# Output product of a hybrid layer: the residual x added by accumulating transfers, the final weight in S1's room, row sums prepared ahead of the last square

## The chip, the cores and the metric

The kernel runs on one core of a Trainium2 chip. The metric is the device time of one execution in microseconds (us). TensorE (PE in the profile) multiplies, VectorE (DVE) and ScalarE (ACT) work elementwise, GpSimd (POOL) and SyncE (SP) mostly issue transfers here. Transfers are issued into queues by SP, ACT and POOL and carried out by 16 DMA engines that all queues share.

## The reference, cut to what matters

One encoder layer: two branches (a Mamba-2 scan and a latent attention), merged by gates, then an output product, the residual and a final RMSNorm. The change touches only the last lines:

```
merged = jax.nn.sigmoid(g_ssm) * (y @ w_proj_ssm) + jax.nn.sigmoid(g_attn) * (o @ w_proj_attn)
x = x + merged @ w_out
...
y = xf * lax.rsqrt(jnp.mean(xf * xf, axis=-1, keepdims=True) + EPS)
return (y * w.astype(jnp.float32)).astype(x.dtype)
```

x and the output have 512 rows (tokens) and 2048 columns, float32.

## The kernel before

All large products are made in split precision: an operand is stored as a high part (rounded to the multiplier's format) and a low part (the remainder), and one product is three matmuls, high by high, high by low and low by high. For weights, ScalarE makes the high part `wh` (L433) and VectorE the low part `wl` (L434), chunk by chunk of 128 x 1024, three buffers deep. So each chunk that TensorE uses needs one ScalarE and one VectorE instruction before it.

The output is made in 128 x 512 tiles, named (t, b): t = 0 to 3 is the block of rows, b = 0 to 3 the block of columns. Columns b = 0 and 1 are multiplied plainly (the loop at L1607 and after). Columns b = 2 and 3 are made by a Strassen scheme (`Strassen.pair`, here called `wo`), with seven products in the order P1, P5, P6, P2, P3, P7, P4. Each is 48 matmuls of 128 x 512 over two banks of PSUM and four weight chunks (m = 0 to 3). Their operands are m's quarters x11, x12, x22 and the sums S1 to S4. P1 uses x11, P5 S1, P6 S2, P2 x12, P3 S4, P7 S3 and P4 x22. X and Y are the weight chunks of the quarter columns, kept and added to: `X<-wo` and `Y<-wo` from POOL's queue are accumulating transfers (L505), which add what they read from memory to what lies in the tile.

What the products leave is combined on VectorE in a tile `big` (parts "p1", "p5", "u", "C12", two tiles each). When P2 has been made, tiles (0, 2) and (1, 2) are complete in p1 (L653). After P3, (0, 3) and (1, 3) are complete in C12 (L630). After P7, (2, 3) and (3, 3) are complete in p5 (L625), and u gets its last addend but one (L728). P4, whose weights are split whole and kept (`keep`), gives (2, 2) and (3, 2) one after the other: first the matmuls of row block 2, then those of 3.

A complete tile goes through `done_o`: the tile of x is added (L1640), the square is summed by ScalarE into `ssf` (L1573), and for t = 2 and 3 the final weight is multiplied in early (`weigh`, L1570). For t = 0 and 1 the tiles of x are loaded by POOL's queue into buffers `gate` ahead of the product (L1628); for t = 2 and 3 they lie, with the final weight, in the tile `fw`, which is loaded by ACT's queue (L1646 and L1649) when P2 is done, in the room that x12 gives up. When a row block is complete, `finish` (L1651) sums its four squares (L1653), scales (L1654), makes the reciprocal root with one Newton step (L185 to L191, one operation on ScalarE and five on VectorE), scales its four tiles and issues their stores.

The program order of each engine is fixed when the kernel is built: TensorE runs in the order of the code, the other engines in an order that a scheduler chooses by priority and data dependences. An engine executes its instructions in order and stops at one whose inputs are not there. Functions hung on a product's name (`hook`) are put into the program when that product has been written down.

Of the kernel before, what the change touches and what calls it, by code (L numbers as in the profile page):

```python
# [18 lines left out]
P = 128  # L19
D = 2048  # L20
# [52 lines left out]
def build(tc, a):  # L73
# [27 lines left out]
    def few(n):  # L101

        n_small[0] += n
        assert n_small[0] <= 96
        return small[:, n_small[0] - n:n_small[0]]
# [275 lines left out]
    def st(name):  # L381
        return gp.tile([P, SEQ], F32, tag="st", bufs=3, name=name)
# [179 lines left out]
    def product(name, op, chunk, extra=None, pre=None):  # L562

        used.append((used[-1] + 1) % 4)
        bs = [b(name) for b in SETS[used[-1]]]
        for m in range(4):
            raw = chunk(m)
            h, l = w_split(raw)
            if extra:
                extra(m, raw)  # L570
            if pre and m == 2:
                pre()
            for i in range(2):
                for jj in range(2):
                    j = 2 * m + jj
                    xh, xl = op(0, j, i), op(1, j, i)
                    wh, wl = (t[:, jj * 512:(jj + 1) * 512] for t in (h, l))
                    pe.matmul(bs[i], xh, wh, start=(j == 0), stop=False)  # L578
                    pe.matmul(bs[i], xh, wl, start=False, stop=False)  # L579
                    pe.matmul(bs[i], xl, wh, start=False, stop=(j == 7))  # L580
                    yield 3
        product_done()
        return bs
# [19 lines left out]
    class Strassen:  # L603
# [60 lines left out]
        def pair(self, cp, headed=False):  # L664
            w, made = self.w, self.made
            X, Y = self.ahead.pop(cp, []), []

            def column(m):
                if m == len(X):
                    X.append(self.columns(w_tile("X"), cp, m))  # L670
                return X[m]

            if headed:
                p1 = self.p1[cp]
            else:
                p1 = evict((yield from product(
                    "P1", self.op("x11"), (lambda m: w_load(w_tile("X"), w, cp, 0, 0, m)) if made else column,
                    None if made else lambda m, raw: w_more(raw, w, cp, 0, 1, m))), "p1", self.tile_)
                self.hook(cp, "P1")

            def c5(m):
                column(m)
                Y.append(w_load(w_tile("Y"), w, cp, 1, 1, m))
                return X[m]

            T3 = []

            def c7(m):
                if made and not T3:
                    T3.extend(t_load(w_tile("Y"), w, cp, "T3", i) for i in range(4))  # L690
                return T3[m] if made else Y[m]

            def t2(m, raw):
                with tc.high_priority(offset=AHEAD):
                    dve.tensor_add(raw, raw, Y[m])

            def t4(m, raw):
                with tc.high_priority(offset=AHEAD):
                    dve.tensor_add(X[m], X[m], raw)

            def t4_alone(m, raw):
                raw = w_tile("w")
                tc.keep_in_program_order(nc.sync.dma_start(raw, a[w][cp, 1, 0, m]))
                t4(m, raw)

            p5 = evict((yield from product("P5", self.op("S1"), c5, t2)), "p5", self.tile_)
            self.hook(cp, "P5")
            A = yield from product("P6", self.op("S2"), lambda m: X[m])
            u = p1 if headed else [self.tile_("u", i) for i in range(2)]
            for i in range(2):  # L710
                dve.tensor_add(u[i], p1[i], A[i])
                self.minus_r(p5[i], p5[i], u[i])
            self.hook(cp, "P6")
            if not headed:
                yield from self.second(cp, p1, lambda i: p1[i], t4)
                self.hook(cp, "P2")
            B = yield from product("P3", self.op("S4"), lambda m: Y[m], None if made else lambda m, raw: w_more(raw, w, cp, 0, 1, m),
                                   self.pre(0, 2 * cp + 1))
            for i in range(2):
                o = sum_tile("ms") if headed else self.tile_("C12" if self.last else "p1", i)  # L720
                self.r_sum(o, p5[i], B[i])
                self.done(i, 2 * cp + 1, o)
            self.hook(cp, "P3")
            A = yield from product("P7", self.op("S3"), c7, t4_alone if headed else None, self.pre(2, 2 * cp + 1))
            for i in range(2):
                self.minus_r(p5[i], p5[i], A[i])
                self.done(2 + i, 2 * cp + 1, p5[i])
                dve.tensor_add(u[i], u[i], A[i])  # L728
            self.hook(cp, "P7")
            if self.last:  # L730
                yield from self.last("P4", self.op("x22"), lambda m: X[m], u)
                return
            A = yield from product("P4", self.op("x22"), lambda m: X[m], None, self.pre(2, 2 * cp))
            for i in range(2):
                self.r_sum(u[i], u[i], A[i])
                self.done(2 + i, 2 * cp, u[i])
            self.hook(cp, "P4")
# [139 lines left out]
    def rsqrt1(v):  # L877

        return small_rsqrt(v, 1, lambda n: hi.tile([P, 1], F32, tag={"rt": "mx", "rr": "nm"}[n], bufs=4, name=n))
# [487 lines left out]

    n_places = [0]

    def place(shape, name):  # L1370

        n = n_places[0] % 5
        n_places[0] += 1
        return xb.tile(shape, F32R, tag="opb" if n else "opc", bufs=4 if n else 1, name=name)

    def slot(which):
        if which in ("x11", "x12"):
# [173 lines left out]
    def x_of(t, b):  # L1551
        return a["x"][t * P:(t + 1) * P, b * SEQ:(b + 1) * SEQ]
# [13 lines left out]
        return w_split(w_load(w_tile("w"), "wo", 0, kc // 4, cg, kc % 4))  # L1566

    def weigh(t, b):
        if t >= 2 and b != 2:
            dve.tensor_mul(res[t, b], res[t, b], room["fw"][:, b])  # L1570

    def squares(t, b):
        act.activation(st("scr"), res[t, b], AF.Square, accum_out=ssf[:, t, b:b + 1])  # L1573

    def m_sums(q):
        ks = slice(4 * q, 4 * q + 4)
# [45 lines left out]
    m_place("S4")()  # L1622
    m_split("S4")()

    def fetch_o(t, b):
        if t < 2:
            fetched[t, b] = st("gate")
            pool.dma_start(fetched[t, b], x_of(t, b))  # L1628

    def kept_o(tag, i):  # L1630
        if "big" not in room:
            room["big"] = xa.tile([P, 4, 2, SEQ], F32, tag="opa", bufs=2, name="big")
        return room["big"][:, ("p1", "p5", "u", "C12").index(tag), i]

    def x_late(t, b):
        return fetched[t, b] if t < 2 else room["fw"][:, 2 * (b - 2) + 2 + t]

    def done_o(t, b, o):
        res[t, b] = o
        dve.tensor_add(o, o, x_late(t, b))  # L1640
        squares(t, b)
        weigh(t, b)

    def final_weights():
        t_ = room["fw"] = xa.tile([P, 8, SEQ], F32, tag="opa", bufs=2, name="fw")
        act.dma_start(t_[:, 0:4], a["fnw"].rearrange("o (b n) -> o b n", b=4).broadcast_to([P, 4, SEQ]))  # L1646
        for t in (2, 3):
            for b in (2, 3):
                act.dma_start(x_late(t, b), x_of(t, b))  # L1649

    def finish(t):  # L1651
        v = few(1)
        dve.tensor_reduce(v, ssf[:, t, :], AX.X, ALU.add)  # L1653
        dve.tensor_scalar(v, v, 1.0 / D, EPS, ALU.mult, ALU.add)  # L1654
        r = rsqrt1(v)
        for b in (2, 0, 1, 3):
            o = res[t, b]
            if b == 2 or t < 2:
                dve.scalar_tensor_tensor(o, o, r, room["fw"][:, b], ALU.mult, ALU.mult)
            elif b == 1 or b == 2:  # L1660
                dve.tensor_scalar_mul(o, o, r)
            else:
                act.activation(o, o, AF.Copy, scale=r)
            (nc.sync if t < 3 or b % 2 == 0 else act).dma_start(a["out"][t * P:(t + 1) * P, b * SEQ:(b + 1) * SEQ], o)

    def last_o(name, op, chunk, u):
        keep = [place([P, 4, 1024], f"keep{i}") for i in range(2)]

        def before():
            for i in range(2):  # L1670
                dve.tensor_add(u[i], x_late(2 + i, 2), u[i])

        def each(i, bank):
            res[2 + i, 2] = u[i]
            with tc.high_priority(offset=12 * i):
                dve.tensor_add(u[i], u[i], bank)
                squares(2 + i, 2)
            finish(2 + i)

        yield from product_rows(name, op, chunk, keep, each, before)  # L1680

    wo = Strassen("wo", m_ops, 1, done_o, fetch_o, {
        (1, "P2"): [final_weights],
        (1, "P3"): [lambda: [weigh(t, b) for t in (2, 3) for b in (0, 1)], lambda: finish(0)],
        (1, "P7"): [lambda: finish(1)]}, kept_o, last_o)
    used.extend([0, 0, 3])
    run(wo.pair(1))
    manual.__exit__(None, None, None)
# [68 lines left out]
```

## Time and profile before

| | |
|---|---|
| median of the three runs shown | 2021.59 us (2018.48 to 2027.99) |
| the profiled execution | 2028.84 us |
| its span, first to last instruction | 2027.1 us |
| mean granted TensorE clock | 0.991 |
| TensorE busy | 1951.1 us (96%) |
| VectorE busy | 1523.9 us (75%) |
| ScalarE busy | 985.2 us (49%) |
| POOL busy | 318.6 us (16%) |
| first matmul of P7 | starts at 1988.14 us |
| last matmul (of P4) | starts at 2016.39 us |
| last store issued | 2022.20 us |

A row of a timeline has the start, the duration, the engine, the line, the operation, the tile written and the tiles read. Square brackets give the time for which the engine had been idle and what ended that. A row of a windows view has, for a stretch of time, the busy us of PE, its weight loads, DVE, ACT and POOL with their counts, then the granted clock, the share of time for which the DMA engines were busy, and GB/s.

### The profile page before, as it was taken

Reading aid. Unit: us, or ns where it says so; the run is one execution under the profiler, and the core shown is the slowest. Engines: PE = TensorE matmul, PEld = TensorE weight load, DVE = VectorE, ACT = ScalarE, POOL = GpSimd, SP = SyncE. Lnnn points to the kernel's source line nnn. Section 1 sums busy time; section 2 is a strip of 40 time slices with the busy share of each in tenths; the row PEclk is TensorE's granted clock in tenths of the full one; section 3 lists DMA queues with packets and bytes.
Section 4 is the critical chain, followed back from the end, with each engine's and each line's share of the span. In section 5 each row is a group of like instructions: output and inputs, shape, how many; then the busy total and the mean of one; then the engine's idle time right before and its main releaser. Section 6 shows DMA issues by size and latency. Waiting matters only on the chain.

```text
span 2027.1 us, 24730 instructions
## 1 busy us (share of the span) xinstructions
PE 1951.1 (96%) x9026; PEld 1610.9 (79%) x9026; DVE 1523.9 (75%) x2010; ACT 985.2 (49%) x1370; POOL 318.6 (16%) x353
## 2 busy tenths in 40 slices
PE   6999999999999999999999999999999999999996
PEld 5888888888878778787788878887877787888885
DVE  7976676676759879899787577666676898879376
ACT  6444445444444655646546444444455455444353
POOL 0001001001032242243331101110011111100010
PEclk9999999999999999999999999999999999999999
DMA  5468558558456747686574857883279787847436
GB/s 192 166 186 208 159 132 208 158 134 208 125 172 170 233 144 209 215 243 201 168 200 149 245 158 197 206 222 94 72 216 301 221 289 281 285 151 244 156 63 176
DMA packets 168650, 382.77 MB, mean 189 GB/s; under 512 B 16272, under 2 KB 65552, under 8 KB 168336
## 3 DMA queue, kind: packets, MB, share of 16 engines
q1 hardware_dynamic: 103248, 233.61, 35.5%
q0 software_dynamic: 29824, 102.25, 22.8%
q10 hardware_dynamic: 35456, 45.33, 6.3%
q8 instruction: 71, 1.16, 0.2%
q14 instruction: 51, 0.42, 0.1%
HBM read 329.22 MB, written 98.04 MB: 211 GB/s over the span
## 4 chain that ended last, share of the span: by engine, by line
PE 60%; DVE 17%; issue 10%; DMA 8%; ACT 3%; POOL 1%; SPq 0%; DVEq 0%; POOLq 0%; ACTq 0%
PE P L579 9%; PE P L580 9%; PE P L578 9%; PE za L168 2%; PE za L169 2%; PE za L170 2%; DVE sum L1052 2%; DVE wl L434 2%; PE xbc L168 2%; PE xbc L169 2%; PE xbc L170 2%; DVE wl L164 2%; DMA wraw<-wps 1%; PE pb L1329 1%; PE qkv L170 1%
## 5 line engine op out<-in xcount | busy, mean ns | idle before, releaser
L433 ACT CAST wh<-X 128x1024 fp32r<-128x1024 f32 x164 | 172.3, 1053 | 197.1 <-PE P L580 149.9
L434 DVE TENSOR_TENSOR wl<-X,wh 128x1024 fp32r<-128x1024 f32 x164 | 199.8, 1222 | 90.5 <-ACT wh L433 90.1
L164 DVE TENSOR_TENSOR wl<-wraw,wh 128x1024 fp32r<-128x1024 f32 (+2 forms) x148 | 176.7, 1195 | 85.4 <-ACT wh L163 83.2
L163 ACT CAST wh<-wraw 128x1024 fp32r<-128x1024 f32 (+2 forms) x150 | 145.1, 969 | 134.2 <-PE xbc L169 39.5
L434 DVE TENSOR_TENSOR wl<-Y,wh 128x1024 fp32r<-128x1024 f32 x88 | 107.3, 1222 | 68.6 <-ACT wh L433 68.6
L168 PE MATMUL xbc<-h_h,wh 128*128 128x512 f32 x384 | 152.8, 398 | 0.0
L433 ACT CAST wh<-Y 128x1024 fp32r<-128x1024 f32 x88 | 92.6, 1054 | 123.4 <-PE P L580 105.5
L169 PE MATMUL xbc<-h_l,wh 128*128 128x512 f32 x384 | 150.8, 393 | 0.0
L170 PE MATMUL xbc<-h_h,wl 128*128 128x512 f32 x384 | 150.7, 392 | 0.0
L578 PE MATMUL P<-wh,h_h 128*128 128x512 f32 x384 | 149.4, 389 | 0.0
L579 PE MATMUL P<-wl,h_h 128*128 128x512 f32 x384 | 149.4, 389 | 0.0
L580 PE MATMUL P<-wh,h_l 128*128 128x512 f32 x384 | 149.4, 389 | 0.0
L434 DVE TENSOR_TENSOR wl<-wraw,wh 128x1024 fp32r<-128x1024 f32 x68 | 83.1, 1221 | 63.3 <-ACT wh L433 63.2
L433 ACT CAST wh<-wraw 128x1024 fp32r<-128x1024 f32 x68 | 71.6, 1053 | 115.9 <-PE P L580 61.8
L579 PE MATMUL P<-wl,S 128*128 128x512 f32 x288 | 112.3, 390 | 0.3 <-DVE wl L434 0.2
L578 PE MATMUL P<-wh,S 128*128 128x512 f32 x288 | 112.1, 389 | 0.0
L580 PE MATMUL P<-wh,S 128*128 128x512 f32 x288 | 112.0, 389 | 0.0
L168 PE MATMUL za<-h_h,wh 128*128 128x512 f32 x256 | 101.4, 396 | 0.0
L169 PE MATMUL za<-h_l,wh 128*128 128x512 f32 x256 | 99.9, 390 | 0.0
L170 PE MATMUL za<-h_h,wl 128*128 128x512 f32 x256 | 99.9, 390 | 0.0
L1052 DVE TENSOR_TENSOR_SCAN sum<-da,scn 128x512 f32<-128x512 f32 x64 | 86.2, 1360 | 0.0
L170 PEld LDWEIGHTS xbc<-h_h,wl 128*128 128x128 f32 x384 | 72.9, 190 | 15.7
(737 smaller groups left out, 5200.5 us busy)
## 6 DMA issues: line engine op xcount, KB each, us to landing
wraw<-wi SPq DMA_DIRECT2D x102, 512.0 KB, 4.2
T_wps<-wps POOLq DMA_DIRECT2D x32, 512.0 KB, 6.3
da<-da_d SPq DMA_DIRECT2D x64, 256.0 KB, 4.5
T_wpa<-wpa POOLq DMA_DIRECT2D x32, 512.0 KB, 9.4
wraw<-wps SPq DMA_DIRECT2D x24, 512.0 KB, 6.0
wraw<-wo SPq DMA_DIRECT2D x20, 512.0 KB, 3.5
xbc_d<-xbc ACTq DMA_DIRECT2D x24, 256.0 KB, 3.0
wraw<-wun SPq DMA_DIRECT2D x16, 384.0 KB, 3.2
```

What stands on the lines that cost most here:

```text
L163: act.copy(h, raw)
L164: (dve if ahead[0] else pool).tensor_sub(l, raw, h.bitcast(F32))
L168: pe.matmul(out, wh, xh, start=start, stop=False)
L169: pe.matmul(out, wh, xl, start=False, stop=False)
L170: pe.matmul(out, wl, xh, start=False, stop=stop)
L433: i = act.copy(hi_, raw)
L434: dve.tensor_sub(lo_, raw, hi_.bitcast(F32))
L578: pe.matmul(bs[i], xh, wh, start=(j == 0), stop=False)
L579: pe.matmul(bs[i], xh, wl, start=False, stop=False)
L580: pe.matmul(bs[i], xl, wh, start=False, stop=(j == 7))
L1052: dve.tensor_tensor_scan(sums[dd], flat(da), mask, 0.0, ALU.add, ALU.mult)
L1329: pe.transpose(tp[:, k * P:(k + 1) * P], prs[t][:, k * P:(k + 1) * P], ident)
```

## The change

Four things change, all in the output product.

1. x is no longer loaded into tiles of its own and added on VectorE. An accumulating transfer of POOL's queue adds it in the parts themselves (`x_added`): into p1 and u after P6, into C12 and p5 after P3. A part holds its final value only with P2's, P7's or P4's banks, so for p1, u and p5 x is in before the last addend; C12 is complete before x comes.
2. The final weight `fw` is loaded after P5 into the room that S1 gives up, by itself. The second half of P4's kept weights moves into x12's room, which is free after P2.
3. The weighing of tiles (2, 0), (3, 0), (2, 1), (3, 1) moves from after P3 to after P2, and `finish` of row blocks 0 and 1, two calls now together, to the last chunk of P7.
4. For row blocks 2 and 3 three of the four squares are summed, scaled and given EPS before the last square (`most`); the last square then goes straight into the root on ScalarE as its input, with `most` as bias. The Newton step takes four VectorE operations instead of five.

```
+            def late(m, raw):
+                if m == 3:
+                    self.hook(cp, "P7a")
...
-    def fetch_o(t, b):
-        if t < 2:
-            fetched[t, b] = st("gate")
-            pool.dma_start(fetched[t, b], x_of(t, b))
...
+    def x_added(tag, t0, b):
+        for i in range(2):
+            pool.dma_start(kept_o(tag, i), x_of(t0 + i, b), accum_op=ALU.add)
 
     def done_o(t, b, o):
         res[t, b] = o
-        dve.tensor_add(o, o, x_late(t, b))
-        squares(t, b)
-        weigh(t, b)
+        if (t, b) == (1, 3):
+            x_added("C12", 0, 3)
+            x_added("p5", 2, 3)
+        if t >= 2 or b == 2:
+            squares(t, b)
+        elif t == 1:
+            for i in range(2):
+                squares(i, b)
+        if t >= 2:
+            weigh(t, b)
 
     def final_weights():
-        t_ = room["fw"] = xa.tile([P, 8, SEQ], F32, tag="opa", bufs=2, name="fw")
...
-        for t in (2, 3):
-            for b in (2, 3):
-                act.dma_start(x_late(t, b), x_of(t, b))
+        room["fw"] = place([P, 8, SEQ], "fw", F32)[:, 0:4]
+        tc.keep_in_program_order(act.dma_start(
+            room["fw"], a["fnw"].rearrange("o (b n) -> o b n", b=4).broadcast_to([P, 4, SEQ])))
...
+    def r_near(v, root):
+        r = few(1)
+        dve.reciprocal(r, root)
+        dve.scalar_tensor_tensor(root, r, r, v, ALU.mult, ALU.mult)
+        dve.tensor_scalar(root, root, -0.5, 1.5, ALU.mult, ALU.add)
+        dve.tensor_mul(r, r, root)
+        return r
...
+    def finish_last(t, most):
+        v, root = few(1), few(1)
+        act.activation(root, ss_of(t, 2), AF.Sqrt, bias=most, scale=1.0 / D)
+        dve.tensor_scalar(v, ss_of(t, 2), 1.0 / D, most, ALU.mult, ALU.add)
+        r = r_near(v, root)
...
-        keep = [place([P, 4, 1024], f"keep{i}") for i in range(2)]
+        keep = [place([P, 4, 1024], "keep0"), xa.tile([P, 4, 1024], F32R, tag="opa", bufs=2, name="keep1")]
...
         def before():
-            for i in range(2):
-                dve.tensor_add(u[i], x_late(2 + i, 2), u[i])
+            most.extend(sums_of(2 + i, 3) for i in range(2))
...
+    wo = Strassen("wo", m_ops, 1, done_o, None, {
+        (1, "P5"): [final_weights],
+        (1, "P6"): [lambda: x_added("p1", 0, 2), lambda: x_added("u", 2, 2)], (1, "P2"): [weigh_first],
+        (1, "P7a"): [lambda: finish(0), lambda: finish(1)]}, kept_o, last_o)
```

How this moves instructions. VectorE before, from the weighing to the first reduction of `finish`; `gate` is a loaded tile of x, `wl<-Y` the splits of P7's four chunks:

```order
L1570 TENSOR_TENSOR p_15492<-p_15492,fw 128x512
L1570 TENSOR_TENSOR kk<-kk,fw 128x512
L1570 TENSOR_TENSOR p_15494<-p_15494,fw 128x512
L1570 TENSOR_TENSOR kk<-kk,fw 128x512
L630 TENSOR_TENSOR big<-big,P_16394 128x512
L1640 TENSOR_TENSOR big<-big,gate 128x512
L434 TENSOR_TENSOR wl<-Y,wh 128x1024 x3
L630 TENSOR_TENSOR big<-big,P_16395 128x512
L1653 TENSOR_REDUCE small<-small 128x1
L1640 TENSOR_TENSOR big<-big,gate 128x512
```

The first L1640 stands ahead of three of P7's splits. VectorE now, from the last weighing to the first reduction of `finish`; the first `wl<-Y` is P3's last chunk, the other four are P7's:

```order
L1573 TENSOR_TENSOR kk<-kk,fw 128x512
L434 TENSOR_TENSOR wl<-Y,wh 128x1024
L434 TENSOR_TENSOR keep_16579<-X,keep_16578 128x1024
L434 TENSOR_TENSOR wl<-Y,wh 128x1024
L434 TENSOR_TENSOR keep_16579<-X,keep_16578 128x1024 x2
L434 TENSOR_TENSOR wl<-Y,wh 128x1024
L630 TENSOR_TENSOR big<-big,P_16392 128x512
L630 TENSOR_TENSOR big<-big,P_16393 128x512
L434 TENSOR_TENSOR wl<-Y,wh 128x1024
L434 TENSOR_TENSOR keep_16579<-X,keep_16578 128x1024
L434 TENSOR_TENSOR wl<-Y,wh 128x1024
L1676 TENSOR_REDUCE small<-small 128x1
```

All additions of x are gone, the splits of P4's weights have moved among P7's, and the reduction stands behind P7's last split. POOL's queue before, its last transfers:

```order
L505 DMA X<-wo 128x1024 x2
L1628 DMA gate<-x 128x512 x2
L505 DMA X<-wo 128x1024 x2
L505 DMA Y<-wo 128x1024 x3
L1628 DMA gate<-x 128x512
L505 DMA Y<-wo 128x1024
L1628 DMA gate<-x 128x512
```

POOL's queue now, the same place:

```order
L505 DMA X<-wo 128x1024 x4
L1640 DMA big<-x 128x512 x4
L505 DMA Y<-wo 128x1024 x4
L1640 DMA big<-x 128x512 x4
```

Four plain loads became eight accumulating ones, four on each side of Y's.

More of the change, by code (lines that the diff above doesn't have):

```diff
@@ L723, in pair @@
             self.hook(cp, "P3")
-            A = yield from product("P7", self.op("S3"), c7, t4_alone if headed else None, self.pre(2, 2 * cp + 1))
+            def late(m, raw):
+                if m == 3:
+                    self.hook(cp, "P7a")
+            A = yield from product("P7", self.op("S3"), c7, t4_alone if headed else late, self.pre(2, 2 * cp + 1))
             for i in range(2):
@@ L1368, in build, with place @@
     n_places = [0]
-    def place(shape, name):
+    def place(shape, name, dt=F32R):
         n = n_places[0] % 5
         n_places[0] += 1
-        return xb.tile(shape, F32R, tag="opb" if n else "opc", bufs=4 if n else 1, name=name)
+        return xb.tile(shape, dt, tag="opb" if n else "opc", bufs=4 if n else 1, name=name)
     def slot(which):
@@ L1568, in weigh, with ss_of @@
     def weigh(t, b):
-        if t >= 2 and b != 2:
-            dve.tensor_mul(res[t, b], res[t, b], room["fw"][:, b])
+        return dve.tensor_mul(res[t, b], res[t, b], room["fw"][:, b])
+    def ss_of(t, b):
+        i = (0, 1, 3, 2)[b]
+        return ssf[:, t, i:i + 1]
     def squares(t, b):
-        act.activation(st("scr"), res[t, b], AF.Square, accum_out=ssf[:, t, b:b + 1])
+        act.activation(st("scr"), res[t, b], AF.Square, accum_out=ss_of(t, b))
     def m_sums(q):
@@ L1633, in kept_o @@
         return room["big"][:, ("p1", "p5", "u", "C12").index(tag), i]
-    def x_late(t, b):
-        return fetched[t, b] if t < 2 else room["fw"][:, 2 * (b - 2) + 2 + t]
+    def x_added(tag, t0, b):
+        for i in range(2):
+            pool.dma_start(kept_o(tag, i), x_of(t0 + i, b), accum_op=ALU.add)
     def done_o(t, b, o):
         res[t, b] = o
-        dve.tensor_add(o, o, x_late(t, b))
-        squares(t, b)
-        weigh(t, b)
+        if (t, b) == (1, 3):
[8 more added lines that the diff above has]
+            weigh(t, b)
@@ L1644, in final_weights, with weigh_first @@
     def final_weights():
-        t_ = room["fw"] = xa.tile([P, 8, SEQ], F32, tag="opa", bufs=2, name="fw")
-        act.dma_start(t_[:, 0:4], a["fnw"].rearrange("o (b n) -> o b n", b=4).broadcast_to([P, 4, SEQ]))
+        room["fw"] = place([P, 8, SEQ], "fw", F32)[:, 0:4]
+        tc.keep_in_program_order(act.dma_start(
+            room["fw"], a["fnw"].rearrange("o (b n) -> o b n", b=4).broadcast_to([P, 4, SEQ])))
+    def weigh_first():
         for t in (2, 3):
-            for b in (2, 3):
-                act.dma_start(x_late(t, b), x_of(t, b))
@@ L1651, in finish @@
-    def finish(t):
[L1652 to L1655, printed above, removed]
+            for b in (0, 1):
+                tc.keep_in_program_order(weigh(t, b))
+    def r_near(v, root):
[5 more added lines that the diff above has]
+        return r
@@ new lines, in sums_of, with out_of @@
+    def sums_of(t, n):
+        v = few(1)
+        dve.tensor_reduce(v, ssf[:, t, 0:n], AX.X, ALU.add)
+        dve.tensor_scalar(v, v, 1.0 / D, EPS, ALU.mult, ALU.add)
+        return v
+    def out_of(t, b, queue):
+        queue.dma_start(a["out"][t * P:(t + 1) * P, b * SEQ:(b + 1) * SEQ], res[t, b])
+    def finish(t):
+        v, root = sums_of(t, 4), few(1)
+        act.activation(root, v, AF.Sqrt)
+        r = r_near(v, root)
+        for b in range(4):
+            o = res[t, b]
+            dve.scalar_tensor_tensor(o, o, r, room["fw"][:, b], ALU.mult, ALU.mult)
+            out_of(t, b, nc.sync)
@@ L1656, in finish @@
+    def finish_last(t, most):
+        v, root = few(1), few(1)
+        act.activation(root, ss_of(t, 2), AF.Sqrt, bias=most, scale=1.0 / D)
+        dve.tensor_scalar(v, ss_of(t, 2), 1.0 / D, most, ALU.mult, ALU.add)
+        r = r_near(v, root)
         for b in (2, 0, 1, 3):
             o = res[t, b]
-            if b == 2 or t < 2:
+            if b == 2:
                 dve.scalar_tensor_tensor(o, o, r, room["fw"][:, b], ALU.mult, ALU.mult)
-            elif b == 1 or b == 2:
+            elif b == 1:
@@ L1663, in finish @@
                 act.activation(o, o, AF.Copy, scale=r)
-            (nc.sync if t < 3 or b % 2 == 0 else act).dma_start(a["out"][t * P:(t + 1) * P, b * SEQ:(b + 1) * SEQ], o)
+            out_of(t, b, nc.sync if t < 3 or b % 2 == 0 else act)
     def last_o(name, op, chunk, u):
-        keep = [place([P, 4, 1024], f"keep{i}") for i in range(2)]
+        keep = [place([P, 4, 1024], "keep0"), xa.tile([P, 4, 1024], F32R, tag="opa", bufs=2, name="keep1")]
+        most = []
         def before():
-            for i in range(2):
-                dve.tensor_add(u[i], x_late(2 + i, 2), u[i])
+            most.extend(sums_of(2 + i, 3) for i in range(2))
         def each(i, bank):
@@ L1677, in each @@
                 squares(2 + i, 2)
-            finish(2 + i)
+            finish_last(2 + i, most[i])
         yield from product_rows(name, op, chunk, keep, each, before)
[L1682 to L1685, printed above, removed]
+    wo = Strassen("wo", m_ops, 1, done_o, None, {
+        (1, "P5"): [final_weights],
+        (1, "P6"): [lambda: x_added("p1", 0, 2), lambda: x_added("u", 2, 2)], (1, "P2"): [weigh_first],
+        (1, "P7a"): [lambda: finish(0), lambda: finish(1)]}, kept_o, last_o)
     used.extend([0, 0, 3])
```

## Prediction

> **What bounds the kernel now.** I read the page first, then TensorE's waits in the last 170 us, then the timeline of all engines around the one that showed up.
>
> The page gives the span:
>
> ```profile
> span 2027.1 us, 24730 instructions
> ```
>
> The profiled execution took 2028.84 us, 1.7 us more than its span and 7.25 us above the median of the runs shown (2021.59, which themselves lie between 2018.48 and 2027.99). I work out a gain on the span and take it off the median. The orders of instructions on all five engines agree up to the start of wo's product, at about 1932 us, so only the last 95 us can differ.
>
> TensorE's waits after 1860 us are one row:
>
> ```profile
> PE P L579 <- DVE wl L434: 5.0, 1, 5.0
> ```
>
> The timeline, all engines, around it (start, duration, engine, line; in brackets the idle time and what ended it):
>
> ```profile
> 1981.62 0.57 POOL L1628 DMA_DIRECT2D gate<-x  x1 [0.34 <-DVE big L1640]
> ...
> 1988.14 0.39 PE L578 MATMUL P<-wh,S__15483 128*128 128x512 f32 x1
> ...
> 1991.61 0.69 DVE L1640 TENSOR_TENSOR big<-big,gate 128x512 f32<-128x512 f32 x1 [3.73 <-DMA gate<-x]
> 1992.22 3.49 DVE L434 TENSOR_TENSOR wl<-Y,wh 128x1024 fp32r<-128x1024 f32 x3
> ...
> 1993.49 0.80 PE L579 MATMUL P<-wl,S__15483 128*128 128x512 f32 x1 [4.96 <-DVE wl L434]
> ...
> 1994.09 0.63 PE L580 MATMUL P<-wh,S__15483 128*128 128x512 f32 x1
> ...
> 1996.63 0.40 PE L580 MATMUL P<-wh,S__15483 128*128 128x512 f32 x1
> ...
> 1998.71 0.63 ACT L1573 ACTIVATE scr<-big 128x512 f32<-128x512 f32 x1
> ...
> 1999.45 1.28 ACT L185 ACT_TABLE_LOAD   x1
> ...
> 2001.95 0.75 DVE L1659 SCALAR_TENSOR_TENSOR big<-big,rr,fw 128x512 f32<-128x512 f32 x1
> ...
> 2002.62 0.74 DVE L1659 SCALAR_TENSOR_TENSOR p<-p,rr,fw 128x512 f32<-128x512 f32 x1
> ```
>
> P7 (operand S3, `S__15483`) starts at 1988.14. Its second matmul needs the low half of a weight chunk, and that split stands on VectorE behind the addition of an x tile (L1640) whose transfer, issued at 1981.62, lands at 1991.6. TensorE loses 5.12 us there (1993.49 against 1988.37), and the matmuls behind start 0.42 us apart instead of 0.227 until 1996.63. TensorE's last matmul:
>
> ```profile
> 2016.39 0.39 PE L599 MATMUL P<-keep,x__15388 128*128 128x512 f32 x1
> ```
>
> From 1988.14 there are 95 steps of 0.227 us to it, 21.57 us, so without stall and slow clock it would start at 2009.71. **The stall costs 6.7 us in all.** Behind TensorE stands a tail on VectorE, its timeline:
>
> ```profile
> 2005.27 0.68 DVE L625 TENSOR_TENSOR big<-big,P 128x512 f32<-128x512 f32 x1
> 2005.87 0.68 DVE L728 TENSOR_TENSOR big<-big,P 128x512 f32<-128x512 f32 x1
> ...
> 2013.26 0.68 DVE L1676 TENSOR_TENSOR big<-big,P 128x512 f32<-128x512 f32 x1
> 2014.79 0.16 DVE L1653 TENSOR_REDUCE small<-small 128x1 f32<-128x4 f32 x1 [0.85 <-ACT scr L1573]
> ...
> 2016.37 0.75 DVE L1659 SCALAR_TENSOR_TENSOR big<-big,rr,fw 128x512 f32<-128x512 f32 x1
> ...
> 2017.44 0.68 DVE L1676 TENSOR_TENSOR big<-big,P 128x512 f32<-128x512 f32 x1
> 2018.97 0.16 DVE L1653 TENSOR_REDUCE small<-small 128x1 f32<-128x4 f32 x1 [0.85 <-ACT scr L1573]
> ...
> 2019.58 0.16 DVE L187 RECIPROCAL rr<-rt 128x1 f32<-128x1 f32 x1 [0.27 <-ACT rt L185]
> 2019.78 0.16 DVE L188 TENSOR_TENSOR rt<-rr 128x1 f32<-128x1 f32 x1
> ```
>
> The two L1676 are the last additions of P4's banks to rows 2 and 3; I call them add 1 and add 2. From add 2 to the end of the span are 9.66 us. Add 2 came 0.6 us after TensorE's end, behind a scaling in row 2's finish.
>
> **The change, part by part.** *The plain x loads go*: four `gate` and four `fw<-x` transfers, and on VectorE eight additions of 0.60 us (the pitch of L625 and L728). With L1640 the wait of P7's start goes. Late next, on VectorE, are the steps ahead of P7's first split. A product is 48 steps of 0.227, 10.9 us, so P3 starts at 1977.25, and from then stand in line: two L653 (P2's banks), four weighings of 0.60 us, two splits for P3 and one of P4's weight, 1.16 us each (3.49 for three). Laid end to end, with the wait for ScalarE's high parts, they bring P7's first split to its end at about 1985.2, 3 us ahead of its need; the next splits end at 1988.6, 1991.0 and 1993.3, wanted at 1990.9, 1993.6 and 1996.3. So TensorE should not wait.
>
> *Eight accumulating transfers come in*, all in POOL's queue. The first two (p1) may leave once P6's banks are added, about 1967; u waits for the subtraction of it from p5:
>
> ```profile
> 1969.60 1.28 DVE L625 TENSOR_TENSOR big<-big 128x512 f32<-128x512 f32 x2
> ```
>
> So the four are issued by about 1972.5. The share of the DMA engines (next to last column) says what they find:
>
> ```profile
> 1954.00:1965.00 11.00, 11.00 (x50) 9.11 (x49) 7.43 (x8) 8.06 (x10) 0.00 (x0) 1.00 0.03 5
> 1965.00:1976.00 11.00, 11.00 (x50) 9.11 (x49) 10.99 (x12) 5.17 (x5) 0.86 (x1) 1.00 0.12 44
> 1976.00:1987.00 11.00, 11.00 (x50) 9.10 (x49) 9.81 (x13) 4.40 (x7) 3.74 (x5) 1.00 1.00 222
> ```
>
> First read at 1977 (L653), they cost nothing, and the final weight, issued behind P5 (ended 1955.5) and first read at 1978, costs nothing either. If the cover failed, L653 would hold P3's third split, one for one after some 2 us. The full stretch 1976 to 1987 is relieved of 2.5 MB (the weight's 128 x 2048 and six tiles of x).
>
> The other four (C12, then p5) are issued when P3's banks have been added, L630 at 1988.6 and 1989.2 behind a split. Two C12 go out at about 1989.4 and 1990.0. **This adds a wait**: ScalarE's squares of rows 0 and 1 wait for them, the table load and roots wait for the squares, and VectorE's reduction of row 0 waits at 1993.3. Queued behind it on VectorE are the eight scalings of rows 0 and 1, P7's four additions, two weighings and add 1. TensorE waits for none of these: P4's weights are split by then.
>
> How long does an accumulating transfer of 256 KB take? DMA issues from 1900 us on (KB each, median us to landing):
>
> ```profile
> X<-wo POOLq DMA_DIRECT2D x4, 512.0 KB, 5.4
> Y<-wo POOLq DMA_DIRECT2D x4, 512.0 KB, 9.7
> ...
> gate<-x POOLq DMA_DIRECT2D x4, 256.0 KB, 7.1
> ```
>
> X and Y are the accumulating ones, Y in the full stretch. All of L505's, by line:
>
> ```profile
> DMA to landing us min/median/max: 5.2/7.1/12.1
> ```
>
> L1357's, which accumulate in DRAM at 256 KB or more:
>
> ```profile
> DMA to landing us min/median/max: 5.0/8.5/21.7
> ```
>
> The plain `gate` loads (L1628):
>
> ```profile
> DMA to landing us min/median/max: 3.6/7.1/11.3
> ```
>
> One `X<-wo` ran alone (windows):
>
> ```profile
> 1926.00:1928.00 2.00, 2.00 (x10) 1.65 (x9) 0.00 (x0) 0.00 (x0) 0.56 (x1) 1.00 0.39 53
> 1928.00:1930.00 2.00, 2.00 (x11) 1.65 (x10) 0.41 (x1) 1.05 (x1) 0.00 (x0) 1.00 1.00 180
> 1930.00:1932.00 2.00, 2.00 (x11) 1.65 (x10) 2.00 (x3) 0.56 (x2) 0.87 (x1) 1.00 0.16 29
> ```
>
> It kept the engines busy for 2 x (0.39 + 1.00 + 0.16) = 3.1 us. Half the bytes give 5.2 - 1.55 = 3.65 us as the lower end for one transfer; the upper end is 21.7. The second C12 stands 0.9 us behind the first one's data. I take 5.5 us for it, near 5.0 and 5.4, since by then nothing else moves: landed at 1995.5.
>
> *Then the chain*, from rows: square and readout to the table load 0.74 us (1998.71 to 1999.45); table load to first scaling 2.50 us (1999.45 to 2001.95), less one step of 0.20, as row 0 and 1's root now takes four small steps instead of five: 1998.55. Eight scalings of 0.67: 2003.9. Six operations of 0.60: 2007.5. Two small reductions, 0.25: add 1 at 2007.7.
>
> *The row sums prepared ahead* take the reduction and the scaling by 1/D out of the path between square and root. The root's row on ScalarE:
>
> ```profile
> 2019.35 0.20 ACT L185 ACTIVATE rt<-small 128x1 f32<-128x1 f32 x1 [0.41 <-DVE small L1654]
> ```
>
> It would start at 2018.97: 0.38 us, and 0.20 for the step saved, 0.58 us per row. Add 1 to add 2 were 4.18 us, now 3.60: add 2 at 2011.3. Add 2 to the end, 9.66 - 0.58 = 9.08: span **2020.4**, a gain of **6.7 us**. TensorE's last matmul ends at 2010.1, so add 2 is now 1.2 us late by VectorE, not by TensorE.
>
> [...] POOL's issues of L505 by target, shortest, median and longest in ns:
>
> ```profile
> L505 POOL DMA_DIRECT2D X<-wz x8: 857/866/1027, 107.8 to 191.9; - x8
> ```
>
> The spread is small beside a VectorE that is busy most of the time. [...]
>
> **The rivals.** *TensorE sets the end*: the C12 land within 4.3 us, add 2 follows TensorE at 2010.15, span 2019.2, gain 7.9 us, median 2013.7. For it: 3.65 + 0.9 is near 4.3. Against it: no accumulating row is under 5.0. The Trainium skill, "DMA: Bandwidth & Descriptors", section "Anatomy of one DMA — SWDGE (gpsimd) path", fits 2.0 us plus bytes over 436 GB/s, 2.6 us here, which would give this case; the plain 256 KB loads of this trace never took under 3.6.
>
> *The C12 land late*: at 9.7 us, as Y<-wo in the full stretch, everything moves by 4.2 us: span 2024.6, gain 2.5, median 2019.1. For it: the four follow Y's in one queue. Against: the stretch is relieved.
>
> *The stall stays under another name*: P7's first splits still come late, through more work ahead of them on VectorE or a late Y. At the full 6.7 us add 2 is at 2016.85, span 2025.9, gain 1.2, median 2020.4. The change then removes a wait and does nothing. Against: 3 us of slack above.
>
> *Slower*: the second C12 stays on its way so long that VectorE's scalings of rows 0 and 1, and all behind them, end later than before. From 12.2 us (5.5 + 6.7) the gain is gone; at 21.7 us the span is 2036.6, 9.5 us longer, median 2031.1. For it: one row reached 21.7. Against: L505's longest is 12.1.
>
> **How the numbers follow.** Forecast 2021.6 - 6.7 = 2014.9 with 0.56; TensorE sets the end 0.20; late C12 0.12; stall stays 0.08; slower 0.04. Half the spread of the runs shown is 4.7 us: the low end is 2013.7 - 4.7 = 2009.0, the high end 2021.5, the stall's case with 1 us. A measurement of this kernel can tell about 0.5% (10.1 us) from no change, and even the best case gains 7.9: faster by more only through scatter, 0.12; slower by more 0.03; within, 0.85.
>
> **What would show it.** Right: no wait of TensorE at P7's start and no 0.42 us matmuls, its last matmul near 2009.7 on this time axis, C12's transfers 5 to 6 us to landing, a VectorE gap of some 2 us before the first reduction, add 2 about 1 us behind TensorE, and 2.5 us, not 3.1, from add 1 to its first scaling. Wrong: a wait of TensorE on `wl` in P3 or P7, an L653 that waits for a transfer, or C12 at 9 us and more. The forecast falls too if the unprofiled runs never had the stall.

## The result, and the profile after

The changed kernel takes 2017.87 us, median of 21 runs, against 2023.03 us for 21 runs of the kernel before: a ratio of 0.9976 with a 95% interval of 0.9965 to 0.9986, some 5 us. In a second set it was 0.9974 (0.9964 to 0.9983). That is faster, by less than 0.5%. One of the 21 executions of the changed kernel took 6695 us; the ratio leaves it out as a slow one, and no run shows what held it.

The two profiled executions differ by more, and part of that isn't the change's. ScalarE's first copy of wo's P1 banks into `big` stands at the same place in both: from it to the first matmul of P7 are 43.32 us before and after. Before:

```profile
1944.82 1.08 ACT L541 COPY big<-P 128x512 f32<-128x512 f32 x2 [1.66 <-PE P L580]
```

After, with the squares of tiles (0,3) and (1,3) and the table load:

```profile
1935.42 1.08 ACT L541 COPY big<-P 128x512 f32<-128x512 f32 x2 [1.66 <-PE P L580]
...
1984.33 0.63 ACT L1581 ACTIVATE scr<-big 128x512 f32<-128x512 f32 x1 [1.61 <-DMA big<-x]
...
1987.38 0.63 ACT L1581 ACTIVATE scr<-big 128x512 f32<-128x512 f32 x1 [2.32 <-DMA big<-x]
...
1988.12 1.28 ACT L1685 ACT_TABLE_LOAD   x1
```

```profile
span 2012.4 us, 24716 instructions
```

This execution comes to that copy 9.40 us earlier, through work that the change doesn't touch (its mean granted clock is 0.996, that of the one before 0.991). From the copy to the end of the span, which I call **the last stretch**, are 82.28 us before and 76.98 after: the change is worth **5.3 us** there, as the medians say. It repeats: two further executions of the changed kernel gave 77.13 and 77.05. Adding 9.40 puts a time of this trace on the prediction's axis.

TensorE's timeline where it had stalled, and its end:

```profile
1978.74 0.39 PE L578 MATMUL P<-wh,S__15483 128*128 128x512 f32 x1
1978.97 0.39 PE L579 MATMUL P<-wl,S__15483 128*128 128x512 f32 x1
1979.19 0.39 PE L580 MATMUL P<-wh,S__15483 128*128 128x512 f32 x1
...
2000.27 0.39 PE L599 MATMUL P<-keep,x__15388 128*128 128x512 f32 x1
```

P7's second matmul follows the first by 0.23 us where it took 5.35, no step of 0.42 us is left, and the last matmul starts at 2000.27, which is 2009.67 on the old axis. Then VectorE's tail:

```profile
1979.18 1.28 DVE L630 TENSOR_TENSOR big<-big,P 128x512 f32<-128x512 f32 x2
...
1985.08 0.16 DVE L1676 TENSOR_REDUCE small<-small 128x1 f32<-128x4 f32 x1 [1.11 <-ACT scr L1581]
...
1988.13 0.16 DVE L1676 TENSOR_REDUCE small<-small 128x1 f32<-128x4 f32 x1 [2.70 <-ACT scr L1581]
...
1990.49 0.75 DVE L1689 SCALAR_TENSOR_TENSOR p<-p,small,fw 128x512 f32<-128x512 f32 x1
...
1995.80 0.68 DVE L625 TENSOR_TENSOR big<-big,P 128x512 f32<-128x512 f32 x1
...
1999.52 0.68 DVE L1717 TENSOR_TENSOR big<-big,P 128x512 f32<-128x512 f32 x1
...
2003.28 0.68 DVE L1717 TENSOR_TENSOR big<-big,P 128x512 f32<-128x512 f32 x1
```

The new wait is there: 3.8 us in two pieces ahead of the two reductions, ended by squares that waited for `big<-x`. The last row, add 2, comes 2.6 us after TensorE's last matmul has ended (2000.66). VectorE sets the end.

### The profile page after: what moved, and what is told of

Its sections match the earlier page's. It is cut to its first block, busy times and chain, and to the rows that moved or that the text cites. A ratio compares the mean times of both kernels' runs of the same rounds, so it can differ in the third digit from the quotient of the medians.

```text
span 2012.4 us, 24716 instructions
## 1 busy us (share of the span) xinstructions
PE 1940.6 (96%) x9026; PEld 1603.2 (80%) x9026; DVE 1520.6 (76%) x2000; ACT 985.2 (49%) x1370; POOL 323.2 (16%) x357
## 4 chain that ended last, share of the span: by engine, by line
PE 70%; DVE 14%; DMA 7%; issue 5%; ACT 3%; POOL 1%; SPq 0%; DVEq 0%; POOLq 0%; ACTq 0%
PE P L579 11%; PE P L580 11%; PE P L578 11%; PE za L168 2%; PE za L169 2%; PE za L170 2%; DVE sum L1056 2%; PE xbc L168 2%; PE xbc L169 2%; PE xbc L170 2%; DVE wl L164 2%; PE f L1565 1%; PE f L1566 1%; PE f L1567 1%; DMA wraw<-wps 1%
## 5 line engine op out<-in xcount | busy, mean ns | idle before, releaser
L1320 ACT ACTIVATE pr<-s,nm 128x512 f32<-128x512 f32 x64 | 44.1, 690 | 83.6 <-DVE nm L1318 82.8
```

The source lines that it names most:

```text
L1320: act.activation(pr, s, AF.Exp, bias=nm, scale=SCALE, accum_out=sm_)
```

## The experiments

Each is read by its last stretch (before 82.28, changed kernel 76.98), since single executions come to its start up to 11.6 us apart (1935.42 us in the changed kernel, 1947.04 in the run of the row sums).

**The two cures of the stall, one at a time.** First the kernel before with the tile `fw` loaded behind P5:

```
-        t_ = room["fw"] = xa.tile([P, 8, SEQ], F32, tag="opa", bufs=2, name="fw")
+        t_ = room["fw"] = place([P, 8, SEQ], "fw", F32)
...
-        (1, "P2"): [final_weights],
+        (1, "P5"): [final_weights],
```

> The kernel before, with only the place and time of the tile `fw` changed: the final weight and the four x tiles of rows 2 and 3 are loaded behind P5 into S1's room and not behind P2; all additions of x stay on VectorE. Theory that the full DMA stretch made the stall: the x load for (0,3) lands in 5 to 7 us instead of 9.9, TensorE does not wait at P7's start, last stretch 75.2 us (7.1 less than before, 1.8 less than the changed kernel, as no accumulating transfer stands in the tail). Rival that the additions of x on VectorE make the stall wherever the loads stand: a TensorE wait of 3 us or more stays, last stretch 79 us or more.

TensorE has no wait in it, the last stretch is 75.68 us, and the ratio to before 0.9979 (0.9963 to 0.9995). Its loads of x for (0,3) and (1,3), by POOL, and what they took to landing:

```profile
1978.07 1.47 POOL L1628 DMA_DIRECT2D gate<-x  x2
```

```profile
DMA to landing us min/median/max: 7.0/7.1/7.2
```

They land in 7.1 us, just over the 5 to 7 named, where the first took 9.9 before. But the scheduler answered the earlier load with another order too: the first of the two additions now stands ahead of one of P7's splits, not of three. So this run alone doesn't say whether landing or place did it. The next one leaves the loads alone and changes VectorE's order: the two additions go behind P7's splits, which are held in the order of the code.

```
         res[t, b] = o
+        if t < 2 and b == 3:
+            return
...
+    def x_behind():
+        for t in range(2):
+            tc.keep_in_program_order(dve.tensor_add(res[t, 3], res[t, 3], x_late(t, 3)))
+            squares(t, 3)
...
+        (1, "P7"): [x_behind, lambda: finish(0), lambda: finish(1)]}, kept_o, last_o)
```

> The kernel before with its loads where they were, and only VectorE's order changed: the additions of x to (0,3) and (1,3) stand behind P7's four splits, and rows 0 and 1 are finished behind P7. Theory (the stall is an addition that waits for a transfer ahead of P7's splits; moving it out of the way is enough, whatever the DMA engines carry): TensorE waits less than 1 us at P7 although the stretch is as full as before, and the last stretch is 77 to 78.5 us, since the scalings of rows 0 and 1 now stand between P4's two additions. Rival (the full stretch makes Y late enough to stall P7 by itself): TensorE waits 3 us or more.

Again TensorE has no wait, with the DMA engines as full as before (busy for a share of 0.98 from 1976 to 1988 us, 1.01 before). VectorE's timeline in it (L436 are the splits, L636 P3's additions, L1661 the moved ones, L1696 P4's):

```profile
1986.25 1.22 DVE L436 TENSOR_TENSOR wl<-Y,wh 128x1024 fp32r<-128x1024 f32 x1
1987.38 0.68 DVE L636 TENSOR_TENSOR big<-big,P 128x512 f32<-128x512 f32 x1
1988.66 0.69 DVE L636 TENSOR_TENSOR big<-big,P 128x512 f32<-128x512 f32 x1 [0.60 <-PE P L586]
1989.27 2.36 DVE L436 TENSOR_TENSOR wl<-Y,wh 128x1024 fp32r<-128x1024 f32 x2
1994.50 1.22 DVE L436 TENSOR_TENSOR wl<-Y,wh 128x1024 fp32r<-128x1024 f32 x1 [2.87 <-ACT wh L435]
...
2002.39 1.29 DVE L1661 TENSOR_TENSOR big<-big,gate 128x512 f32<-128x512 f32 x2
...
2005.65 0.68 DVE L1696 TENSOR_TENSOR big<-big,P 128x512 f32<-128x512 f32 x1
...
2012.63 0.68 DVE L1696 TENSOR_TENSOR big<-big,P 128x512 f32<-128x512 f32 x1
```

The splits come in time; what is left over is at the end, where the scalings of rows 0 and 1 now stand between P4's two additions: 78.36 us. The third run takes a part of the relief out of the changed kernel: the weight, 1 MB, is loaded behind P2 again, and its four weighings go back behind P3.

> The changed kernel, with the final weight loaded behind P2 (into the same room) and the four early weighings moved back behind P3. Theory (the stall came from an x addition that stood ahead of P7's splits; with none there a full DMA stretch only delays Y): TensorE waits less than 1.5 us in all, last stretch 77 to 78.5 us. Rival (the relief of the full stretch is what removes the stall): TensorE waits 3 us or more at P7, last stretch 80 us or more.

No wait of TensorE either, and the last stretch is 75.90 us, 1.1 less than the changed kernel, which neither side expected. VectorE shows why. P3's additions start 43.03 us behind the copy of P1 in it, 43.76 in the changed kernel, because the weighings now stand behind them and not ahead; so C12's transfers leave 0.7 us earlier. Its rows:

```profile
1982.23 1.28 DVE L630 TENSOR_TENSOR big<-big,P 128x512 f32<-128x512 f32 x2
1983.43 0.69 DVE L1573 TENSOR_TENSOR p<-p,fw 128x512 f32<-128x512 f32 x1
```

The second C12 landed 6.9 us after POOL's first issue, where the changed kernel has 7.2. That 0.3 us needn't be the edit's: over the runs that leave these transfers as they are it is 7.0 to 7.4.

One thing follows that the forecast didn't have: by the last stretch, moving the loads of `fw` alone (75.68 us) does better than the whole change (76.98). The ratios, 0.9979 and 0.9976, don't tell the two apart.

**What sets the new end.** In the next kernel nothing is accumulated into C12: x is loaded there plainly behind P1, p5 added behind P6, P3's bank last.

```
-            x_added("C12", 0, 3)
...
+    def x_first():
+        for i in range(2):
+            act.dma_start(kept_o("C12", i), x_of(i, 3))
+
+    def c12_first():
+        for i in range(2):
+            dve.tensor_add(kept_o("C12", i), kept_o("C12", i), kept_o("p5", i))
```

> The changed kernel, but x for tiles (0,3) and (1,3) is loaded plainly into C12's room behind P1, p5 is added to it behind P6, and P3's bank last; nothing is accumulated into C12. I call 'the last stretch' the time from the first copy of P1's banks into `big` to the end of the span: 82.3 us before, 77.0 us in the changed kernel. Theory (the wait for the second accumulated C12 makes VectorE late and sets the end): the wait of VectorE ahead of the first reduction goes, the last addition follows TensorE's last matmul within 0.2 us, last stretch 74.4 us (2.6 less than the changed kernel). Rival (the scalings of rows 0 and 1 would be late anyway, through the table load and the sums): 77.0 us, last addition 2 us or more behind TensorE.

The last stretch is 74.21 us. VectorE:

```profile
1989.41 0.21 DVE L1686 TENSOR_REDUCE small<-small 128x1 f32<-128x4 f32 x2
...
2005.17 0.69 DVE L1727 TENSOR_TENSOR big<-big,P 128x512 f32<-128x512 f32 x1 [1.44 <-PE P L599]
```

The reductions have no wait ahead of them, and add 2 waits for TensorE (its last matmul starts at 2004.75). The ratio to before is 0.9961 (0.9947 to 0.9974). Measured again with more executions, beside the changed kernel:

> The kernel with x loaded plainly into C12's room, in more rounds, beside the changed kernel on the same chip. Theory: ratio to before 0.9960 (8.1 us of 2023, the difference of the last stretches, 82.3 - 74.2), below the changed kernel's 0.9974 (82.3 - 77.0). Rival (what is gained in the last stretch is lost in the spread of the rest): no difference from the changed kernel.

> The changed kernel, on the same chip and against the same runs of before: ratio 0.9974 by the last stretches.

0.9964 (0.9951 to 0.9977) against 0.9974 (0.9964 to 0.9983), last stretches 74.28 and 77.05. By the trace this is the better version, by 2.8 us; the medians point the same way, but their intervals overlap.

Now the other direction, p5's transfers ahead of C12's:

> The changed kernel, with p5's two accumulating transfers ahead of C12's two in POOL's queue. Theory (the landing of the second C12 sets the end): it lands as the last of the four, about 10 us after P3's additions where it was 7.2, and the last stretch grows one for one, to 78.5 to 79.8 us. Rival that the end does not hang on C12: 77.0 us.

79.81 us. ScalarE's squares wait in it until 1993.13 and 1994.39:

```profile
1993.13 0.63 ACT L1581 ACTIVATE scr<-big 128x512 f32<-128x512 f32 x1 [6.25 <-DMA big<-x]
...
1994.39 0.63 ACT L1581 ACTIVATE scr<-big 128x512 f32<-128x512 f32 x1 [0.54 <-DMA big<-x]
```

POOL issued the first of the four at 1984.32, so the second C12 landed 10.05 us after that, where it was 7.19 in the changed kernel: 2.9 us later, and the last stretch grew by 2.8. The end hangs on it one for one.

**Why the second C12 takes so long.** p5's transfers wait for the first square, through a small multiplication on POOL:

```
+            tc.keep_in_program_order(pool.tensor_mul(pace, ss_of(0, 3), ss_of(0, 3)))
+            x_added("p5", 2, 3)
```

> The changed kernel, with p5's two accumulating transfers issued only when the square of tile (0,3) is there, by a small multiplication on POOL that reads it; C12's two go alone. Theory that p5's transfers share the DMA engines with the second C12: that one lands 5.3 us after its issue instead of 6.4, last stretch 75.9 us (1.1 less than the changed kernel), and p5 is there before P7's banks. Rival (6.4 us is what a second accumulating transfer in a queue takes): landing 6.4 us, last stretch 77.0 us.

75.65 us. POOL issued C12's two at 1984.49, and the squares:

```profile
1988.72 0.63 ACT L1581 ACTIVATE scr<-big 128x512 f32<-128x512 f32 x1 [1.66 <-DMA big<-x]
...
1990.38 0.63 ACT L1581 ACTIVATE scr<-big 128x512 f32<-128x512 f32 x1 [0.94 <-DMA big<-x]
```

The second landed 5.9 us after the first issue. Since a microsecond could be chance, both kernels were run again:

> The changed kernel once more, to see how far the last stretch and the landing of the second C12 repeat. Theory (both are set by the program): last stretch 77.0 us within 0.4, second C12 landed 6.9 to 7.3 us after POOL issued the first. Rival (they scatter by a us or more, and the single looks at one change tell little).

> The kernel with p5's transfers issued later, once more. Theory: last stretch 75.65 us within 0.4, second C12 landed 5.9 us after POOL issued the first. Rival (the first look at it was scatter): 77.0 us.

The changed kernel gave 77.13 us and a landing of 7.4, just outside what I had named; the other 75.88 us and 6.2. The difference stands: p5's two, issued right behind, cost the second C12 about 1.3 us.

**The row sums.** The kernel before with this part alone, and the changed kernel without it:

```
+        act.activation(root, ss_of(t, 2), AF.Sqrt, bias=most, scale=1.0 / D)
+        dve.tensor_scalar(v, ss_of(t, 2), 1.0 / D, most, ALU.mult, ALU.add)
```

> The kernel before, with only the row sums of rows 2 and 3 prepared ahead and the root taken straight from the last square. Theory: the stall of 5 us stays, from the first of P4's additions to the second 3.7 to 3.8 us instead of 4.18, or the second follows TensorE; last stretch 81.2 us (1.1 less than before). Rival that the row sums carry most of the change's gain: 78 us or less.

> The changed kernel, with only the root of rows 2 and 3 taken as before (sum of four squares, scaling, five small steps). Theory: 0.42 us later at the last addition and 0.5 us from there to the end: last stretch 77.9 us (0.9 more than the changed kernel). Rival that the table load or the sums hide it: 77.0 us.

81.26 us alone, and 77.74 without. In the first of the two TensorE's stall is 4.0 us and not 5.0, but that isn't where the microsecond comes from: add 1 starts 68.4 us behind the copy of P1 both in it and before. The two additions in it:

```profile
2015.42 0.67 DVE L1716 TENSOR_TENSOR big<-big,P 128x512 f32<-128x512 f32 x1
...
2019.17 0.68 DVE L1716 TENSOR_TENSOR big<-big,P 128x512 f32<-128x512 f32 x1
```

From add 1 to add 2 are 3.75 us (4.18 before), from there to the end 9.13 (9.66). So the part is worth 1.0 us where it is added. Where it is taken out, the same two steps grow by 0.41 and 0.69 us, while add 1 comes 0.34 us earlier: 0.8 in all.

## Why the prediction was right, and by how much it was off

*The time.* 2014.9 us was forecast and 2017.87 measured. Of the 3.0 us, 1.4 lie in the median of before, 2021.59 over three executions and 2023.03 over 21; the rest is the gain, 6.7 forecast and 5.2 measured by the medians, 5.3 by the traces. The mechanism held; one term of the sum, C12's landing, was too small.

*The stall.* Right: no wait at P7, no slow matmuls, the last matmul at 2009.67 against 2009.71 forecast. P7's splits end at 1975.9, 1979.3, 1981.6 and 1984.0, on the old axis 1985.3, 1988.7, 1991.0 and 1993.4, where 1985.2, 1988.6, 1991.0 and 1993.3 were laid out. That the relief of the full stretch plays a part, the prediction left open; the runs show that it isn't needed: with the weight late there is no stall, and with every load in its old place the order alone ends it. Nor did the DMA engines fall idle in that stretch: they are busy for a share of 1.03 from 1966 to 1978 us in the changed kernel, where it was 1.01 from 1976 to 1988 before. But Y, with less beside it, landed in 6.3 us (median) where it took 9.7:

```profile
Y<-wo POOLq DMA_DIRECT2D x4, 512.0 KB, 6.3
```

*The first four accumulations and the weight* cost nothing, as forecast; no instruction waited for them.

*C12.* This is the term that was mis-sized. Issue at 1989.4 and 1990.0 was forecast, 1989.56 and 1990.35 were measured; the landing of the second was put at 5.5 us and took 6.4. The POOL row and the landings of all eight (shortest, median, longest):

```profile
1980.16 3.50 POOL L1640 DMA_DIRECT2D big<-x  x4 [5.48 <-DVE big L630]
```

```profile
DMA to landing us min/median/max: 4.1/6.1/8.1
```

The prediction took 5.5 us because "by then nothing else moves". It left out p5's two, which it had itself put right behind in the same queue; with these held back the second C12 took 5.1 and 5.4 us from its own issue, so 5.5 would have done. With the later issue, 0.35 us, it landed 1.25 us late. From there the chain went as laid out: 0.74 us to the table load, 2.37 to the first scaling (2.30), 5.31 for eight scalings, 3.72 to add 1 (3.85), 3.76 to add 2 (3.60) and 9.12 to the end (9.08). On the old axis the span is 2021.8 against 2020.4: 5.3 us gained, not 6.7. The signs named for this part were off with it: VectorE's gap ahead of the reductions is 3.8 us and not some 2, and add 2 comes 2.6 us behind TensorE and not about 1.

*The row sums* gave 0.42 us instead of 0.58 ahead of add 2 (4.18 to 3.76). The root that takes its bias from a tile took longer than the old one, and so did the step that does two multiplications (L1669, 0.22 us where L188 and L189 took 0.16 each):

```profile
2001.05 0.29 ACT L1694 ACTIVATE small<-small 128x1 f32<-128x1 f32 x1
```

0.29 us where the old one took 0.20.

*The rivals.* "TensorE sets the end" didn't happen, but its price was right: with C12 out of the way the gain is 82.28 - 74.21 = 8.1 us, 7.9 were worked out. "The stall stays" and "slower" are out. "The C12 land late" is the direction in which it went, by 1.25 of its 4.2 us. One reading there was too narrow: 3.6 us is the shortest plain 256 KB load of POOL's queue (`gate`); SP's loads of `da` in the same trace, 256 KB too, took 3.2 us at the least.

## What to carry to other kernels

When a wait in the middle of a kernel goes, lay out the tail behind it with what the change has put there: here 6.7 us came free on TensorE, but a chain over VectorE, POOL, DMA and ScalarE set the new end 2.6 us behind it, and 5.3 us were gained. If an addition that waits for a transfer stands ahead of work that the bottleneck needs, moving it in the order takes the wait away as well; what is moved then has to be paid for at its new place: here the scalings came between P4's two additions, and the last stretch was 78.36 us against 75.68. Here the transfer that set the end came 1.3 us sooner with nothing issued right behind it, and the end 2.8 us sooner where the addend that was known early was loaded before the last operand and not added after it.

## What the runs showed of the hardware

Here a transfer is delayed by those that are issued behind it in the same queue. The DMA engines in the changed kernel, from the issue of the four (the share is the last but one column):

```profile
1980.00:1982.00 2.00, 2.00 (x11) 1.65 (x10) 2.00 (x3) 0.34 (x1) 1.84 (x3) 1.00 0.10 16
1982.00:1984.00 2.00, 2.00 (x11) 1.65 (x10) 1.95 (x2) 0.72 (x1) 1.66 (x2) 1.00 0.82 137
1984.00:1986.00 2.00, 2.00 (x11) 1.65 (x10) 0.31 (x2) 0.72 (x2) 0.00 (x0) 1.00 0.82 125
1986.00:1988.00 2.00, 2.00 (x10) 1.69 (x9) 0.00 (x0) 0.62 (x2) 0.00 (x0) 1.00 1.05 186
1988.00:1990.00 2.00, 2.00 (x10) 1.65 (x9) 0.67 (x6) 1.68 (x5) 0.00 (x0) 1.00 0.38 72
```

Four transfers keep them busy for 6.3 us, 1.6 each, as half of a 512 KB one would. They landed in the order of their issue, but not 1.6 us apart: the second 3.05 us after the first, the third and fourth 1.3 and 1.5 us after the one ahead. When p5's two were held back, the second landed 1.66 and, run again, 1.94 us after the first. That the four share the engines is the likely reading; how the engines shared the work isn't to be seen in these traces.
